# Four banks of the output projection begun early, and v rearranged in 2 KB rows

## The chip, the cores and the metric

The kernel runs on one core of a Trainium2 chip. The metric is the device time of one execution in microseconds, lower is better. Before the change three runs took 482.67, 484.89 and 485.15 us, median 484.89. TensorE (PE) multiplies 128x128 stationary weights by up to 512 moving columns into PSUM, which has eight banks of 128 x 512 float32 here; VectorE (DVE), ScalarE (ACT) and GpSimd (POOL) work beside it; nearly all DMAs are issued in order by SyncE (SP). Each engine runs its own instructions in a fixed order.

## The reference

One encoder layer on 1024 tokens of width 1024. A projection, two kinds of windowed attention, a gate, an output projection, a layer norm:

```python
h = x @ w_in                                   # columns split into eight sections
q_a, k_a, v_a, z_a, q_b, k_b, v_b, z_b = split(h)
# group a: 16 x 64 grid of tokens, 8 heads; each token sees an 8 x 16 window, with a bias per head
y_a = neighborhood_attention(q_a, k_a, v_a, rel_bias)
# group b: 8 query heads on 2 key heads, |i - j| <= 128, rotary positions, a sink logit per head
y_b = windowed_gqa_with_sink(rotary(q_b), rotary(k_b), v_b, sink)
mixed = concat([y_a * silu(z_a), y_b * silu(z_b)])
y = mixed @ w_out                              # 1024 x 1024
out = layer_norm(alpha * x + y) * gain + bias
```

## The kernel before

**Number format.** Float32 products are made from two halves. A tensor `r` is split into `h = round(r)` and `l = r - h`, and a product takes three matmuls: h·h, h·l and l·h. So each weight tile needs a cast (mostly ScalarE) and a subtraction (mostly GpSimd, 128x512) before PE can use it. `w_split` does this for the 42 tiles of `w_in` (`wr` raw, `wh`, `wl` split), `wo_split` for the 16 tiles of `w_out` (`wor` raw, `woh`, `wol`), `m_queue` and `m_split` for the eight 128-row slices `mh[e]`, `ml[e]` of the gated attention output.

**Stages.** First v is projected for all tokens (line 360) and scaled; `vt` holds its two float16 halves. Line 443 writes v of group a to DRAM as `vd`, 4 head pairs x 1024 tokens x 256 values (512 bytes a token and pair). Line 447 copies from it, in four DMAs, the column windows of the 16-row grid that four blocks of queries need, into `vwin0` to `vwin3` (24, 32, 32 and 24 columns of each grid row). Later `gather_v` (line 464) loads one block of one pair into `va`: partition = (row within a group of four, column), and four groups of rows side by side, 512 bytes each. That is once per pair and block, 16 loads, the last four in steps 112 to 118.

Before the step loop six projections (`zb0`, `z0`, `zb1`, `kb`, `qb0`, `z1`) run in full. `w_split(m)` also asks for the load of tile `m + 3` (line 137) once tile `m` is split. The scheduler orders the engines in this first part; the order in the step loop is that of the program.

**The step loop.** 128 units of attention (64 of group b, then 64 of group a; one unit is 128 queries of one head) run as a pipeline. Step `i` does the score matmuls of unit `i` (`stage_qk`, lines 531 and 532, into a bank with tag `s`, of which there are three), the masked copy and maximum on VectorE (line 538), the exponential on ScalarE (line 554), and for unit `i - 1` the split of the probabilities into float16 halves (ScalarE line 564, VectorE line 565) and their transpose by a DMA (line 568, into `tr`). Every fourth step, 8 steps late, the probabilities of four units are multiplied with v (`stage_pv`, line 593, 36 matmuls in group a) and four steps after that transposed and gated (`stage_ot`, lines 613 and 622).

Between these the loop fills PE with other work: the other 15 projections (48 matmuls each, line 290), then the first part of the output projection, called heads. `FILL_AT` gives the steps between which each piece of work is spread evenly, `FILL_N` its number of matmuls. The last projection is `z3`, 48 matmuls over steps 112 to 120. After it come five heads of nine matmuls: bank `(t, a)` holds 128 tokens `t` by 512 columns `a` of the output, and a head adds the slices e = 4, 5, 6 (group b), three matmuls each, into `(0, 0)`, `(1, 0)` (tag `pj`), `(3, 0)`, `(2, 0)`, `(0, 1)` (tag `s`), at steps 120 to 134. PE's matmuls of the output projection are all on line 702 (`out_mms`).

ScalarE, VectorE, GpSimd and SyncE have queues of small jobs (`enq`); in each step `pop` emits a fixed number of those whose predecessors are out. `wo_load` (line 656) asks for a tile of `w_out`; nine raw buffers exist. `WO_LD` gives the steps of the loads inside the loop (111 to 131), the splits come three steps later for tiles 0 to 5, `M_AT` the steps at which the slices e = 4, 5, 6 are split.

**The last stage** (`final`) loads tiles 9 to 14, splits the slices 7, 0, 1, 2, 3 and the tiles 6 to 15, begins banks `(1, 1)`, `(2, 1)`, `(3, 1)` with slices 4 to 6, adds the five slices to eight banks (t = 0 to 3), then does t = 4 to 7 in full. `residual` and `norm` (layer norm, in halves on VectorE, ScalarE and GpSimd) follow each row block; `norm_last` ends the kernel.

Of the kernel before, what the change touches and what calls it, by code (L numbers as in the profile page):

```python
# [9 lines left out]
F16 = mybir.dt.float16  # L10
# [7 lines left out]
GW = 64  # L18
ROWS = 16
# [8 lines left out]
         "k2", "q2", "z2", "k3", "q3", "z3"]  # L28
NPRO = 6
FILL = ORDER[NPRO:]  # L30
FILL_AT = [0, 8, 17, 25, 33, 41, 49, 57, 66, 74, 81, 89, 97, 105, 112, 120, 123, 126, 128, 131, 134]
ZTAG = {"z3": "zv", "zb3": "zc", "z2": "zs"}
X1AT = 4
VA_AT = [50, 53, 56, 59]
WO_TAG = ("wr", "wr", "wr", "wh", "wl", "wh", "wl", "wh", "wl")
M_AT = [105, 112, 115]
WO_LD = [111, 112, 113, 121, 122, 123, 129, 130, 131]
WIN0 = (0, 8, 24, 40)
WINW = (24, 32, 32, 24)
NKEY = tuple(12 * w for w in WINW)  # L40
# [6 lines left out]
def hybrid_block(ctx, tc, xT, x, wt, wv, wo, bias, sink, gain, lbias, cos, sin, bmask, out):  # L47
    nc = tc.nc
# [6 lines left out]
    dram = ctx.enter_context(tc.tile_pool(name="dram", bufs=1, space=bass.MemoryType.DRAM))  # L55
# [3 lines left out]
    def bank(tag):  # L59
        bufs = {"pj": 2, "s": 3, "t": 2, "ot": 1}[tag]  # L60
        return (ps1 if bufs == 1 else ps2).tile([128, 512], F32, tag=tag, name=f"ps_{tag}", bufs=bufs)

    vd = dram.tile([4, S, 256], F16, name="vd")
    vwin = [dram.tile([4, ROWS, WINW[b] * 256], F16, name=f"vwin{b}") for b in range(4)]

    def half_tile(name):
        return big.tile([128, 512], F32R, tag="big", name=name)
# [42 lines left out]
    def enq(eng, fn, *deps, prio=1):  # L110
        op = Op(eng, fn, deps, prio)
        if clock["step"] is None:
            op.emit()
        else:
            queues[eng].append(op)
        return op
# [15 lines left out]
    NH = 2 * len(ORDER)  # L132
# [26 lines left out]
    w_ops, stk_ops, load_ops = {}, {}, {}  # L159
# [113 lines left out]
    def new_group():  # L273
        if len(groups) >= 2:
            need(*groups[-2])
        return bank("pj")
# [35 lines left out]
    with ExitStack() as vctx:  # L312
# [131 lines left out]
                vd[:, 128 * t:128 * t + 128, :].rearrange("q p e -> p q e"),  # L444
                vt[:, 0:8].rearrange("p (q h) i e -> p q (h i e)", h=2))
        for b in range(4):
            nc.sync.dma_start(vwin[b], vd.rearrange("q (r c) e -> q r (c e)", c=GW)[
                :, :, 256 * WIN0[b]:256 * (WIN0[b] + WINW[b])])

# [8 lines left out]
    def gather_v(p, b):  # L460
        w = WINW[b]
        t = ap.tile([128, 4, 256], F16, tag="va", name=f"va{p}_{b}", bufs=5)
        bulk["last"] = bulk["step"]
        nc.sync.dma_start(t[:4 * w], vwin[b][p].rearrange("(g i) (c e) -> (i c) g e", g=4, e=256))
        va[p, b] = t

    def unit_list():
# [155 lines left out]

    pump_all(ORDER[1:NPRO])
    fill.extend(project(n) for n in FILL)
    FILL_N = [48] * len(FILL) + [9] * 5
    pumped = [0]

    def pump_to(u):
# [10 lines left out]
    def m_alloc(e, pair):  # L640
        mh[e], ml[e] = (stk(pair) for _ in range(2))
# [2 lines left out]
        hi(mh[e][:, sl], zt[e][:, sl])  # L644
        lo(ml[e][:, sl], zt[e][:, sl], mh[e][:, sl].bitcast(F32))

    WO_SEQ = [(e, a) for a in range(2) for e in EO[:3]] + [(e, a) for e in EO[3:] for a in range(2)]
    wo_parts = {}

    wo_raw = {}  # L650
# [1 line left out]
    def wo_load(n):  # L652
        if n < 16:
            raw = wp.tile([128, 512], F32, tag=WO_TAG[n % 9], name=f"wor{n}", bufs=3)
            e, a = WO_SEQ[n]
            nc.sync.dma_start(raw, wo[e, :, 512 * a:512 * a + 512])
            wo_raw[n] = raw
# [3 lines left out]
    def wo_split(n):  # L661
        def hi():
            wo_parts[n] = [half_tile(f"wo{w}{n}") for w in "hl"]
            copy = nc.vector.tensor_copy if clock["step"] is None else nc.scalar.copy
            copy(wo_parts[n][0], wo_raw[n])  # L665

        def lo():
            h, l = wo_parts[n]
            eng.tensor_sub(l, wo_raw.pop(n), h.bitcast(F32))  # L669

        eng, q = (nc.vector, "dve") if n % 3 == 2 else (nc.gpsimd, "pool")
        o = enq("act" if clock["step"] is not None else "dve", hi, load_ops.get(("wo", n)))
        o = enq(q, lo, o)
        wo_ops[n] = o
        if n >= 6:
            wo_load(n + 9)

    m_ops = {}

# [11 lines left out]
    def out_mms(t, a, ps, es, c=None):  # L691
        w = 512 if c is None else 256
        o = 0 if c is None else 256 * c
        ts, cs = slice(128 * t, 128 * t + 128), slice(o, o + w)
        ps = ps[:, o:o + w]
        for e in es:
            n = WO_SEQ.index((e, a))
            if n in wo_ops:
                need(wo_ops[n], *m_ops.get(e, ()))
            woh, wol = wo_parts[n]  # L700
            for i, (lh, rh) in enumerate(((mh[e], woh), (mh[e], wol), (ml[e], woh))):
                nc.tensor.matmul(ps, lh[:, ts], rh[:, cs],  # L702
                                 start=(e == EO[0] and i == 0), stop=(e == EO[-1] and i == 2))
                yield

    obank = {}

    def out_head(t, halves, tag):
        for a in halves:
            if tag == "pj":  # L710
                obank[t, a] = new_group()
                groups.append([])
            else:
                obank[t, a] = bank(tag)
        for e in EO[:3]:
            for a in halves:
                yield from out_mms(t, a, obank[t, a], [e])

    def final():
        actx.close()  # L720
        fp = ctx.enter_context(tc.tile_pool(name="fp", bufs=2, reuse_waits="tile"))
        eps = fp.tile([128, 1], F32, name="eps", bufs=1)
        nc.vector.memset(eps, EPS)
        m_alloc(7, "k")
        m_alloc(0, "k")
        m_alloc(1, "q")
        for e in (2, 3):
            mh[e] = fp.tile([128, S], F32R, name=f"mh{e}", bufs=1)
            ml[e] = fp.tile([128, S], F32R, name=f"ml{e}", bufs=1)
        for n in range(9, 15):  # L730
            wo_load(n)
        for e in EO[3:]:
            m_split(e, slice(0, 512), nc.scalar.copy, nc.vector.tensor_sub)
            for n in (WO_SEQ.index((e, 0)), WO_SEQ.index((e, 1))):
                wo_split(n)
        for e in EO[3:]:
            m_split(e, slice(512, S), nc.scalar.copy, nc.vector.tensor_sub)
        gb, bb = zslot("gb"), zslot("bb")
        nc.sync.dma_start(gb, gain.partition_broadcast(128))
# [62 lines left out]

        for t in range(NX):
            x_load(t)
        for t, a, tag in ((1, 1, "t"), (2, 1, "t"), (3, 1, "ot")):
            obank[t, a] = bank(tag)
            list(out_mms(t, a, obank[t, a], EO[:3]))
        for e in EO[3:]:
            for t in range(4):
                for a in range(2):  # L810
                    list(out_mms(t, a, obank[t, a], [e]))
                    if e == EO[-1]:
                        residual(t, a, obank[t, a])
                        if a == 0 and t > 0:
                            norm(t - 1)
                            x_load(t - 1 + NX)
# [13 lines left out]
        for c in range(2):  # L830
            ps = bank(next(tags) if c == 0 else "pj")
            list(out_mms(7, 1, ps, EO, c))
            residual(7, 1, ps, c)
        norm_last(7)

    fill.extend(out_head(t, (a,), tag) for t, a, tag in ((0, 0, "pj"), (1, 0, "pj"), (3, 0, "s"), (2, 0, "s"), (0, 1, "s")))
    clock["step"] = 0
    with tc.manual_schedule():
        for i in range(-LD, NU + LO):
            if 0 <= i + LD < NU:  # L840
                stage_load(units[i + LD])
            if i < 0:
                continue
            clock["step"] = i
            per, h = divmod(i, 16)
            bulk["step"] = i
            if i in VA_AT:
                gather_v(0, VA_AT.index(i))
            if i in WO_LD:
                n = WO_LD.index(i)  # L850
                load_ops["wo", n] = enq("sp", lambda n=n: wo_load(n))
            if i - 3 in WO_LD[:6]:
                wo_split(WO_LD.index(i - 3))
            if i in M_AT:
                m_queue(4 + M_AT.index(i))
            if bulk["last"] != i or (queues["sp"] and i - queues["sp"][0].born > 2):
                pop("sp", 1)
            if i < NU:
                u = units[i]
                if u[3] in (0, (0, 0)) and u[2] == 0:  # L860
                    need(*stk_ops[f"b{u[1]}" if u[0] == "b" else u[1]])
                stage_qk(u)
            q, m = divmod(i - LP - 3, 4)
            if m == 0 and 0 <= q - 1 < NU // 4:
                stage_ot(q - 1)
            if m == 0 and 0 <= q < NU // 4:
                stage_pv(q)
            if 0 <= i - LT < NU:
                stage_tr(units[i - LT])
            pump_to(i + F1)  # L870
            if m in (0, 2) and 0 <= q < NU // 4:
                g, p, j, h = quad(q)
                if g == "a" and j == 1 and p < 3:
                    gather_v(p + 1, 2 * h + m // 2)
            if m == 1 and 0 <= q < NU // 4:
                stage_on(q)
            pop("dve", ND if i < M_AT[1] else 2)
            if i < NU:
                stage_exp(units[i])
            pop("act", NA if i < M_AT[0] else 2)  # L880
            pop("pool", NP)
            pump_to(i + 1)
        pump(10 ** 6)
        need(*[op for q in queues.values() for op in q])
        clock["step"] = None
        final()


# [71 lines left out]
```

## Time and profile before

| what | us |
|---|---|
| median of three runs | 484.89 |
| the profiled execution, its own time | 485.24 |
| its span (first to last instruction) | 483.4 |
| PE busy in the span | 467.9 |
| v projection, on PE alone (line 360) | to about 62 |
| copies to `vwin` issued (line 447) | 102.84 to 105.62 |
| first scores (step 0) | 121.02 |
| scores of step 112 / 120 / 127 | 353.92 / 370.39 / 386.37 |
| end of the last matmul | about 475.4 |
| issue of the last store | 480.45 |

A window row of the profile gives, for a stretch of time, the busy time and number of instructions of each engine, the granted TensorE clock (1.00 is full speed), the mean busy share of the 16 DMA engines (it can exceed 1, where packets overlap) and the rate. A timeline row gives start, duration, engine, line, operation and tiles, and in brackets how long the engine had been idle and what released it. In a list of waits the three numbers are the total, how many times, and the longest. "DMA to landing" is from a DMA's issue to its last byte.

### The profile page before, as it was taken

How to read it: one execution, taken by the hardware profiler on the slowest of the kernel's cores; microseconds unless marked ns; L12 is line 12 of the kernel's file. 1: busy time of each engine (PE TensorE's matmuls, PEld its weight loads, DVE VectorE, ACT ScalarE, POOL GpSimd, SP SyncE). 2: the span in 40 equal slices, each digit the busy share in tenths (PEclk: the TensorE clock that was granted, in tenths of full speed). 3: DMA queues.
4: the chain of work that ended last, by engine and by line, in shares of the span. 5: the costliest groups of instructions: out<-in, count | busy, mean ns of one | idle time of the engine just before them, and what ended most of it. 6: DMA issues, size and time to landing. Idle time of an engine off the chain costs nothing.

```text
span 483.4 us, 9130 instructions
## 1 busy us (share of the span) xinstructions
PE 467.9 (97%) x3240; PEld 402.4 (83%) x3240; DVE 328.1 (68%) x780; ACT 251.2 (52%) x595; POOL 163.1 (34%) x151
## 2 busy tenths in 40 slices
PE   8999999999999999999999999999999599999993
PEld 6999988888788888888888888888888488888883
DVE  5728305868677878888788767767667549569445
ACT  5651123343577867777677766666777532012002
POOL 0030012596245247473215124113634116215423
PEclk9999999999999999999999999999999989999998
DMA  7871001477176666575999998999999988005612
GB/s 238 270 250 44 1 0 45 135 247 245 49 116 114 147 128 121 101 135 117 179 163 187 190 227 190 234 187 264 180 169 228 201 242 279 36 24 159 204 50 87
DMA packets 132381, 74.73 MB, mean 155 GB/s; under 512 B 101104, under 2 KB 117488, under 8 KB 132080
## 3 DMA queue, kind: packets, MB, share of 16 engines
q1 hardware_dynamic: 132192, 74.00, 67.0%
q8 instruction: 25, 0.41, 0.4%
q14 instruction: 20, 0.16, 0.1%
q10 hardware_dynamic: 144, 0.15, 0.1%
HBM read 43.72 MB, written 9.96 MB: 111 GB/s over the span
## 4 chain that ended last, share of the span: by engine, by line
PE 89%; DVE 4%; DMA 3%; ACT 2%; issue 1%; SPq 0%; ACTq 0%; DVEq 0%
PE ps_pj L290 44%; PE ps_s L702 7%; PE ps_t L593 7%; PE ps_t L702 5%; PE ps_pj L702 4%; PE ps_s L531 4%; PE ps_s L360 4%; PE ps_s L532 4%; PE ps_pj L360 3%; PE ps_t L360 3%; DMA tr<-split 2%; PE ps_ot L702 2%; PE ps_ot L613 1%; PE ps_ot L360 1%; DMA xraw<-in_xT 1%
## 5 line engine op out<-in xcount | busy, mean ns | idle before, releaser
L290 PE MATMUL ps_pj<-xh,wh 128*128 128x512 f32 x336 | 133.9, 398 | 0.8 <-ACT rp_raw L233 0.5
L290 PE MATMUL ps_pj<-xl,wh 128*128 128x512 f32 x336 | 131.9, 392 | 0.0
L290 PE MATMUL ps_pj<-xh,wl 128*128 128x512 f32 x336 | 131.6, 392 | 0.0
L152 POOL TENSOR_TENSOR wl<-wr,wh 128x512 fp32r<-128x512 f32 x42 | 55.5, 1323 | 170.7 <-ACT wh L148 129.6
L554 ACT ACTIVATE ps_s<-sn,nm 128x385 f32<-128x385 f32 (+3 forms) x128 | 70.5, 551 | 56.7 <-DVE nm L538 55.5
L565 DVE SCALAR_TENSOR_TENSOR split<-ps_s,split 128x384 f16<-128x384 f32 (+2 forms) x128 | 65.7, 513 | 17.9 <-ACT split L564 17.3
L290 PEld LDWEIGHTS ps_pj<-xh,wl 128*128 128x128 f32 x336 | 63.1, 188 | 13.3
L290 PEld LDWEIGHTS ps_pj<-xh,wh 128*128 128x128 f32 x336 | 63.2, 188 | 10.8 <-DVE z L262 0.7
L290 PEld LDWEIGHTS ps_pj<-xl,wh 128*128 128x128 f32 x336 | 63.2, 188 | 9.4
L564 ACT ACTIVATE split<-ps_s 128x384 f16<-128x384 f32 (+2 forms) x128 | 58.0, 453 | 10.4 <-DMA tr<-split 8.8
L538 DVE CUSTOM_DVE_ANT_0 sn<-ps_s,bm,nsk 128x384 f32<-128x384 f32 (+1 forms) x64 | 37.2, 582 | 18.9 <-PE ps_s L532 18.1
L538 DVE CUSTOM_DVE_ANT_0 sn<-ps_s,bias 128x288 f32<-128x288 f32 (+1 forms) x64 | 32.4, 506 | 25.3 <-PE ps_s L532 22.5
L531 PE MATMUL ps_s<-ks,qs 128*128 128x384 f32 (+2 forms) x128 | 41.4, 323 | 3.9 <-DVE split L565 3.9
L532 PE MATMUL ps_s<-ks,qs 128*128 128x384 f32 (+2 forms) x128 | 41.3, 322 | 0.0
L215 POOL CAST ks<-ks 64x512 fp32r<-64x512 f32 x40 | 27.2, 679 | 35.0 <-ACT ks L205 18.6
L593 PEld LDWEIGHTS <-tr 128*128 128x128 f16 (+1 forms) x1104 | 36.1, 99 | 2.4 <-issue 1.3
L531 PEld LDWEIGHTS ps_s<-ks,qs 128*128 128x128 f32 x128 | 24.1, 188 | 10.6 <-DVE split L565 5.4
L148 ACT CAST wh<-wr 128x512 fp32r<-128x512 f32 x42 | 25.7, 611 | 11.1 <-PE ps_pj L290 8.5
L532 PEld LDWEIGHTS ps_s<-ks,qs 128*128 128x128 f32 x128 | 24.2, 189 | 5.0
L669 POOL TENSOR_TENSOR wol<-wor,woh 128x512 fp32r<-128x512 f32 x11 | 15.8, 1443 | 35.5 <-ACT woh L665 19.0
L554 ACT ACTIVATION_READ_ACCUMULATOR ps_s<-sn,nm 128x1 f32 x128 | 24.1, 188 | 0.0
L799 POOL TENSOR_TENSOR xr<-xr,gb 128x512 f32<-128x512 f32 x7 | 9.1, 1294 | 42.3 <-ACT xr L796 42.3
(191 smaller groups left out, 865.9 us busy)
## 6 DMA issues: line engine op xcount, KB each, us to landing
wr<-in_wt SPq DMA_DIRECT2D x42, 256.0 KB, 3.1
bias<-in_bias SPq DMA_DIRECT2D x16, 288.0 KB, 4.0
wor<-in_wo SPq DMA_DIRECT2D x16, 256.0 KB, 4.8
xr<-in_x SPq DMA_DIRECT2D x8, 512.0 KB, 6.2
xraw<-in_xT SPq DMA_DIRECT2D x15, 256.0 KB, 4.3
out<-xr SPq DMA_DIRECT2D x14, 256.0 KB, 3.4
bias<-in_bias SPq DMA_DIRECT2D x8, 384.0 KB, 4.6
wvraw<-in_wv SPq DMA_DIRECT2D x7, 320.0 KB, 4.6
```

What stands on the lines that cost most here:

```text
L152: nc.gpsimd.tensor_sub(l, raws.pop(m), h.bitcast(F32))
L215: nc.gpsimd.tensor_copy(t[o, sl], t[a, sl])
L290: nc.tensor.matmul(ps, a[:, k % 4, :], b[half, k], start=(k == 0 and i == 0), stop=(k == KT - 1 and i == 2))
L360: nc.tensor.matmul(ps[:, :320], lh[t // 4, k][:, ts], rh[k][:, cs], start=(k == 0 and i == 0), stop=(k == KT - 1 and i == 2))
L531: nc.tensor.matmul(ps[:, :n], q, sl[0], start=True, stop=False)
L532: nc.tensor.matmul(ps[:, :n], q, sl[1], start=False, stop=True)
L538: nc.vector.tensor_tensor_reduce(sn[:, :n], ps[:, :n], bias_t, -1.0, init, op0=ALU.add, op1=ALU.min, accum_out=nm)
L554: nc.scalar.activation(pt[:, :m], sn[:, :m], AF.Exp, bias=nm, scale=-1.0, accum_out=sm[:, k:k + 1])
L564: nc.scalar.activation(hl[:, :m, 0, :c], src, AF.Copy, scale=PSCALE)
L565: nc.vector.scalar_tensor_tensor(hl[:, :m, 1, :c], src, PSCALE, hl[:, :m, 0, :c], op0=ALU.mult, op1=ALU.subtract)
L593: nc.tensor.matmul(ps[:, HD * m:HD * m + HD], a, b_, start=(i == 0), stop=(i == len(mms) - 1))
L702: nc.tensor.matmul(ps, lh[:, ts], rh[:, cs], start=(e == EO[0] and i == 0), stop=(e == EO[-1] and i == 2))
```

## The change

1. **v.** `vwin[b]` is now, for each pair, `4w` rows of 2 KB: row (i, c) holds the four row groups g side by side, so that `gather_v` reads one piece of 2 KB for each partition instead of four of 512 bytes. The copies into it are 16 instead of 4 (block x pair), and their pattern on both sides runs over g, i, c in this order, with pieces of 512 bytes at the destination.
2. **The last projection and the heads.** `z3` is spread over steps 112 to 123. The heads then go by pairs of banks: `(0,0)` and `(1,0)` (tag `pj`, steps 123 to 128), `(2,0)` and `(3,0)` (tag `s`, 128 to 132), slices 4 to 6; then slice 7 for all four (132 to 135): 18, 18 and 12 matmuls. The four other banks, `(0..3, 1)`, take slices 4 to 7 at the start of the last stage.
3. **Splits.** Slice 7 is split in the loop, from step 121. The order of the tiles (`WO_SEQ`) follows the four slices. Tiles 0 to 3 are split at steps 115, 116, 117 and 125 and tiles 4 to 7 at 132 and 133, by ScalarE and GpSimd (every third by VectorE); their loads are at 111, 112, 113, 122, 129, 129, 130, 130, and tiles 8 to 12 are loaded at 131 to 133. Loads now wait in the queue for the splits that free their buffers, and from step 129 SyncE takes three jobs a step instead of one. The last stage splits the tiles 8 to 15 and slices 0 to 3.
4. **The end.** 20 matmuls of 384 columns on two free banks are issued before `norm_last`; nothing reads their result.

```diff
-FILL_AT = [..., 105, 112, 120, 123, 126, 128, 131, 134]
+FILL_AT = [..., 105, 112, 123, 128, 132, 135]
-M_AT = [105, 112, 115]
-WO_LD = [111, 112, 113, 121, 122, 123, 129, 130, 131]
+M_AT = [105, 112, 115, 121]
+WO_AT = [115, 116, 117, 125, 132, 132, 133, 133]
+WO_LD = [111, 112, 113, 122, 129, 129, 130, 130, 131, 132, 132, 133, 133]
...
-    vwin = [dram.tile([4, ROWS, WINW[b] * 256], F16, name=f"vwin{b}") for b in range(4)]
+    vwin = [dram.tile([4, 4 * WINW[b], 4 * 256], F16, name=f"vwin{b}") for b in range(4)]
...
         for b in range(4):
-            nc.sync.dma_start(vwin[b], vd.rearrange("q (r c) e -> q r (c e)", c=GW)[
-                :, :, 256 * WIN0[b]:256 * (WIN0[b] + WINW[b])])
+            for q in range(4):
+                nc.sync.dma_start(
+                    vwin[b][q].rearrange("(i c) (g e) -> g i c e", i=4, g=4),
+                    vd[q].rearrange("(g i c) e -> g i c e", g=4, i=4)[:, :, WIN0[b]:WIN0[b] + WINW[b], :])
...
-        nc.sync.dma_start(t[:4 * w], vwin[b][p].rearrange("(g i) (c e) -> (i c) g e", g=4, e=256))
+        nc.sync.dma_start(t[:4 * w].rearrange("p g e -> p (g e)"), vwin[b][p])
...
-    FILL_N = [48] * len(FILL) + [9] * 5
+    FILL_N = [48] * len(FILL) + [18, 18, 12]
...
-    WO_SEQ = [(e, a) for a in range(2) for e in EO[:3]] + [(e, a) for e in EO[3:] for a in range(2)]
+    WO_SEQ = [(e, a) for a in range(2) for e in EO[:4]] + [(e, a) for e in EO[4:] for a in range(2)]
...
-        if n >= 6:
-            wo_load(n + 9)
+        if 4 <= n < 7:
+            load_ops["wo", n + 9] = enq("sp", lambda: wo_load(n + 9), o)
...
-    def out_head(t, halves, tag):
-        for a in halves:
+    def out_head(ts, es, tag):
+        for t in ts:
             if tag == "pj":
-                obank[t, a] = new_group()
+                obank[t, 0] = new_group()
                 groups.append([])
-            else:
-                obank[t, a] = bank(tag)
-        for e in EO[:3]:
-            for a in halves:
-                yield from out_mms(t, a, obank[t, a], [e])
+            elif tag is not None:
+                obank[t, 0] = bank(tag)
+        for e in es:
+            for t in ts:
+                yield from out_mms(t, 0, obank[t, 0], [e])
...
-        m_alloc(7, "k")
...
-        for n in range(9, 15):
-            wo_load(n)
-        for e in EO[3:]:
+        for e in EO[4:]:
             m_split(e, slice(0, 512), nc.scalar.copy, nc.vector.tensor_sub)
...
-        for t, a, tag in ((1, 1, "t"), (2, 1, "t"), (3, 1, "ot")):
-            obank[t, a] = bank(tag)
-            list(out_mms(t, a, obank[t, a], EO[:3]))
-        for e in EO[3:]:
+        for t, tag in ((0, "s"), (1, "t"), (2, "t"), (3, "ot")):
+            obank[t, 1] = bank(tag)
+            list(out_mms(t, 1, obank[t, 1], EO[:4]))
+        for e in EO[4:]:
...
+        pa, pb = bank("s"), bank("s")
+        for _ in range(2):
+            for i in range(4):
+                nc.tensor.matmul(pa[:, :384], mh[2][:, :128], wo_parts[14][0][:, :384], start=True, stop=True)
+            for i in range(6):
+                r = slice(64 * (i % 2), 64 * (i % 2) + 64)
+                nc.tensor.matmul((pa, pb)[i % 2][:, :384], mh[2][r, :128], wo_parts[14][0][r, :384],
+                                 start=True, stop=True)
         norm_last(7)
-    fill.extend(out_head(t, (a,), tag) for t, a, tag in ((0, 0, "pj"), (1, 0, "pj"), (3, 0, "s"), (2, 0, "s"), (0, 1, "s")))
+    fill.extend((out_head((0, 1), EO[:3], "pj"), out_head((2, 3), EO[:3], "s"), out_head(range(4), EO[3:4], None)))
...
-            if i in WO_LD:
-                n = WO_LD.index(i)
-                load_ops["wo", n] = enq("sp", lambda n=n: wo_load(n))
-            if i - 3 in WO_LD[:6]:
-                wo_split(WO_LD.index(i - 3))
+            for n in range(len(WO_LD)):
+                if WO_LD[n] == i:
+                    load_ops["wo", n] = enq("sp", lambda n=n: wo_load(n), w_ops.get(NH - 3 + n), wo_ops.get(n - 9))
+            for n in range(len(WO_AT)):
+                if WO_AT[n] == i:
+                    wo_split(n)
...
-                pop("sp", 1)
+                pop("sp", 1 if i < WO_LD[4] else 3)
```

More of the change, by code (lines that the diff above doesn't have):

```diff
@@ L30 @@
 FILL = ORDER[NPRO:]
-FILL_AT = [0, 8, 17, 25, 33, 41, 49, 57, 66, 74, 81, 89, 97, 105, 112, 120, 123, 126, 128, 131, 134]
+FILL_AT = [0, 8, 17, 25, 33, 41, 49, 57, 66, 74, 81, 89, 97, 105, 112, 123, 128, 132, 135]
 ZTAG = {"z3": "zv", "zb3": "zc", "z2": "zs"}
@@ L804, in final @@
             x_load(t)
-        for t, a, tag in ((1, 1, "t"), (2, 1, "t"), (3, 1, "ot")):
-            obank[t, a] = bank(tag)
-            list(out_mms(t, a, obank[t, a], EO[:3]))
-        for e in EO[3:]:
+        for t, tag in ((0, "s"), (1, "t"), (2, "t"), (3, "ot")):
+            obank[t, 1] = bank(tag)
+            list(out_mms(t, 1, obank[t, 1], EO[:4]))
+        for e in EO[4:]:
             for t in range(4):
```

## The prediction

> **What bounds the kernel now.** I read the page first: TensorE is busy almost everywhere, and the chain that ended last runs through it.
>
> ```profile
> PE 467.9 (97%) x3240; PEld 402.4 (83%) x3240; DVE 328.1 (68%) x780; ACT 251.2 (52%) x595; POOL 163.1 (34%) x151
> PE 89%; DVE 4%; DMA 3%; ACT 2%; issue 1%; SPq 0%; ACTq 0%; DVEq 0%
> ```
>
> So time is won only where PE stands still or runs slowly, and anything that holds PE back is lost in full. Second, the windows of the last steps and PE's waits there (columns: window, busy us and count of PE, PEld, DVE, ACT, POOL, granted clock, DMA share, GB/s).
>
> ```profile
> 354.00:370.00 16.00, 16.00 (x140) 13.62 (x139) 11.22 (x33) 12.74 (x34) 8.92 (x7) 1.00 1.10 218
> 370.00:386.40 16.40, 11.43 (x116) 8.96 (x114) 10.36 (x30) 9.31 (x28) 1.27 (x1) 0.94 1.15 204
> 386.40:391.20 4.80, 4.80 (x44) 3.98 (x44) 1.98 (x6) 4.12 (x10) 1.28 (x1) 0.50 0.79 182
> ...
> PE ps_s L531 <- DVE split L565: 3.9, 2, 2.9
> ```
>
> The reader sees PE full until 370 us, then 5.0 us idle in 16.4, then 4.8 us at a granted clock of 0.50, which loses 2.4 us. Together 7.4 us: the most that the rearranged late steps can win. PE waits for a score bank, which waits for the split of an earlier unit, which waits for its transpose. Third, therefore, SyncE's queue there.
>
> ```profile
> 366.70 0.57 SPq L508 DMA_DIRECT2D bias<-in_bias  x1
> 367.38 1.21 SPq L568 DMA_TRANSPOSE tr<-split  x1
> 368.64 0.58 SPq L464 DMA_DIRECT2D va<-vwin  x1
> 369.32 1.56 SPq L568 DMA_TRANSPOSE tr<-split  x1
> 370.93 0.57 SPq L508 DMA_DIRECT2D bias<-in_bias  x1
> 371.60 1.21 SPq L568 DMA_TRANSPOSE tr<-split  x1
> 372.87 0.57 SPq L464 DMA_DIRECT2D va<-vwin  x1
> ```
>
> SyncE issues without a pause: eight transposes from 358.08 to 375.6 us are 2.19 us apart, while the steps come every 2.06 us (scores of step 112 at 353.92, of step 120 at 370.39). Fourth, the place where v is rearranged in DRAM (SyncE, then ScalarE, PE and windows).
>
> ```profile
> 102.84 2.78 SPq L447 DMA_DIRECT2D vwin<-vd  x4
> 106.67 24.00 SPq L137 DMA_DIRECT2D wr<-in_wt  x5
> ...
> 120.74 0.62 ACT L148 CAST wh<-wr 128x512 fp32r<-128x512 f32 x1
> 121.27 0.58 ACT L233 COPY rp_raw<-ps_pj 128x512 f32<-128x512 f32 x1
> ...
> 121.90 0.50 PE L290 MATMUL ps_pj<-xh,wh 128*128 128x512 f32 x1 [0.49 <-ACT rp_raw L233]
> ...
> 91.50:94.00 2.50, 2.50 (x12) 2.07 (x12) 1.11 (x2) 1.17 (x3) 2.22 (x3) 1.00 1.04 314
> 103.30:118.00 14.70, 14.70 (x66) 12.17 (x66) 12.99 (x17) 5.47 (x9) 12.83 (x15) 1.00 0.92 299
> ```
>
> The four vwin copies keep the DMA engines full from 103.3 to 118.0 us. The weight load issued at 106.67 lands 11.9 us later (the longest landing of that line), at 118.6: behind them. ScalarE casts it at 120.74, and in its fixed order the copy of a projection bank (121.27), for which PE waits at 121.90, stands behind that cast. There is about 2 us between the end of the vwin data and a stall of PE.
>
> **The change part by part.** *Late steps.* From the scores of step 112 to those of step 127 before took 386.37 - 353.92 = 32.45 us. PE issues 62 matmuls of 512 columns there instead of 70 (48 of z3 and 14 of the heads instead of 22), at 0.229 us from start to start 14.2 us; 15 score pairs at 0.32 are 4.7, four blocks of probabilities times v and transposes at 1.5 are 6.0; sum 24.9. Steps 112 to 120 keep SyncE's eight transposes, three biases, four gathers and weight loads, so I leave them at 16.5 us although PE needs 13.6. Steps 120 to 127 hold 27 matmuls (6.2), 7 score pairs (2.2), two blocks (3.0): 11.4 us; SyncE needs only 7 x 1.27 + 0.66 + 0.6 = 10.2, as two weight loads have left. A new wait comes in: both pj banks are now opened at step 123, and the second needs the evacuation of z3's second half at once; before, that took from 370.39 to 375.75 us, hidden by the first bank's nine matmuls. Three matmuls (0.7) and a score pair cover it now; I take 1.0 (0 to 3). Scores of step 127 then come at 16.5 + 11.4 + 1.0 = 28.9, 3.55 us earlier. The eight matmuls come later, +1.8. Idle time is spread in pieces under 1 us, where before 2.89 us in one piece came ahead of the slow clock, so I take the 2.4 of slow clock as gone, less 0.3 inside the 32.45: -2.1.
>
> Weights 4 to 7 are now loaded behind the last transpose. That was issued 3.5 us after the last scores; +1.25, three more issues of 0.6, landing 4.8 (its row), a ScalarE cast 0.6, GpSimd's three subtractions in turn at 1.28 to 1.5: the last is ready 13.5 us after the last scores. PE wants it after 34 matmuls (7.8), two v blocks (2.1), transposes (1.3), scores (0.3) and nine head matmuls (2.1): 13.6. Just in time; 0.5 (0 to 2). Late steps together: -3.55 + 1.8 - 2.1 + 0.5 = -3.35, say -3.5 with a trifle for the shorter gathers; bounds -7.4 and +1.
>
> *At nothing:* m7's two casts (0.62) replace two weight casts on ScalarE, and its subtractions find POOL busy 1.27 us of 16.4. The four output banks at full depth have 48 matmuls (11 us) before the first weight split in the last stage is wanted, where 27 were. The 20 matmuls of 384 columns at the end (0.18 us apart by the score rows) run 3.6 us from 475.1 to 478.7, while the last store is issued at 480.45; at half clock they end at 482.3, still inside the span of 483.4. The matmuls taken into the heads are the same work elsewhere.
>
> *v in 2 KB pieces.* Gathers: 112 pieces instead of 448 on average, off PE's path; 0 to -0.5 us, inside the trifle. Their price is the copies: 16 instead of 4, in 112 columns x 16 rows x 4 pairs = 7168 pieces of 512 B, 3.67 MB as before. Issue: 16 x 0.65 = 10.4 us, until 113.3, hidden since the data run to 118 anyway. What decides is on how many DMA engines they run. Before, each had 64 equal rows (q and r are evenly spaced); every other transfer here has 96 or 128 and the windows show all 16 engines filled (share 0.92 to 1.04). The new pattern leads with g, four entries, on both sides; no row shows a lead under 64. Bounds: sixteen engines, 14.7 us as now, cost 0; or a transfer handed out by its leading entries, thus four engines. Then: vd's copies, also of 512 B, moved 314 to 346 GB/s on 16 engines (half-microsecond windows at 92 to 93 us: 345), 21.6 GB/s or 23.7 ns a piece on one; 7168 / 4 x 23.7 ns = 42.5 us, from 103.3 to 145.8. The weight load behind them has a quarter of its rows on those engines and lands about 1.2 us later, 147; cast 0.6, bank copy 0.6, PE goes on at 148.7 instead of 121.9: +26.8. A PE idle that long comes back at the slow clock: +2.4 by the row at 386.4. Sum +29.2. By the vwin rate (299 GB/s: 27.4 ns) the copies take 49.1 us, +6.6; at the best windows (389 GB/s) 37.7, -4.8; if the bank copy is put ahead of the cast PE stops only at 130.2, -8.
>
> I take four engines: four leading entries can't be dealt out evenly to sixteen, and nothing in the trace argues for a second level of splitting. The Trainium skill, "DMA: Bandwidth & Descriptors", section "Why a DMA increments its semaphore by 16 and not by 1", says the same outright: the number of engines is the largest one up to 16 that divides the slowest dimension of both sides, and it is the lowest-numbered ones that are used. By that rule the sum is 510.9; by the rows' share of one it is 481.7. No run here shows a transfer with such a lead.
>
> **Sum.** The profiled execution took 485.24 us (span 483.4 and 1.8 around it), 0.35 above the median of 484.89. 485.24 - 3.5 + 29.2 = 510.9, by the median 510.6.
>
> **The rivals.** *Sixteen engines*, the other side: only the late steps tell, 484.89 - 3.5 = 481.4 (477.5 to 486). For it: the same bytes ran at share 0.92 before. Against: the leading four. It decides as long as the vwin data end by about 120 us. *Sixteen engines and no late gain*: SyncE paces steps 112 to 127 as before (2.19 us a transpose) and the evacuation at 123 costs 3: 484.9 + 1 = 486. *Four engines, but two weight loads are issued ahead of the copies*: the next one is wanted at about 144, with the second projection after 130; 147 + 2 - 144 is 5, so 484.9 - 3.5 + 5 = 486.5. Against: the copies waited only for vd, ready at 102.8, and the load for a buffer freed at 106.65.
>
> **Chances.** Four engines 0.60; sixteen with gain 0.24; sixteen without 0.08; four with loads ahead 0.08. Predicted 510.6; its own range 495 to 521 (-8 - 4.8 - 3 and +6.6 + 4). The whole range reaches from 478 to 521. Half a per cent, 2.4 us, is about what can be told from no change: faster 0.25, same 0.07 (parts of the last two and of the second), slower 0.68.
>
> **What would show it.** Right: DMA share near 0.25 from 104 to 145 us, SyncE's weight loads landing past 140, PE idle from 122 with the wait at a bank copy or a cast of wr, slow clock after it; then the same step spacing as before, and in the last steps no idle over 1 us and no slow clock. Wrong: vwin data done by 120 us and PE full there. The late part is wrong if the scores of step 127 come over 31 us after those of step 112, or if PE waits over 2 us for wol ahead of the four heads.

## The result and the profile after

| kernel | median of the runs, us | lowest to highest |
|---|---|---|
| before (6 runs beside the change) | 483.91 | 482.09 to 485.41 |
| after (6 runs) | 514.35 | 512.44 to 517.58 |

The ratio is 1.0643, 95% interval 1.0597 to 1.0689: 30.4 us slower by the medians. The profiled execution of after took 517.58 us (span 515.8), the longest of its six, 3.2 us above the median. The page again first: total busy time, the row of PE in 40 slices of 12.9 us, the chain that ended last.

```profile
PE 474.3 (92%) x3260; PEld 407.1 (79%) x3260; DVE 324.6 (63%) x776; ACT 253.4 (49%) x597; POOL 165.6 (32%) x153
...
PE   8999999994039999999999999999999798999996
...
PE 77%; SPq 9%; DMA 6%; DVE 4%; ACT 2%; issue 2%; POOL 1%; ACTq 0%; POOLq 0%
```

PE has a hole in the tenth to twelfth slice (4, 0, 3), 116 to 155 us, that wasn't there. The chain has a new member, SyncE's issuing queue, with 9% of the span (46 us); before it had 0%. The place is where v is rearranged, so its rows come next: SyncE, then ScalarE and PE from the timeline (start, duration, engine, line; in brackets the idle time and its releaser), then the windows.

```profile
103.62 39.77 SPq L449 DMA_DIRECT2D vwin<-vd  x16
143.49 15.74 SPq L138 DMA_DIRECT2D wr<-in_wt  x5
...
149.32 0.62 ACT L149 CAST wh<-wr 128x512 fp32r<-128x512 f32 x1 [27.96 <-DMA wr<-in_wt]
149.85 0.58 ACT L234 COPY rp_raw<-ps_pj 128x512 f32<-128x512 f32 x1
...
150.48 0.79 PE L291 MATMUL ps_pj<-xh,wh 128*128 128x512 f32 x1 [28.42 <-ACT rp_raw L234]
```

```profile
106.00:122.00 16.00, 16.00 (x72) 13.06 (x70) 13.82 (x16) 5.90 (x10) 11.65 (x12) 1.00 0.29 87
122.00:143.00 21.00, 0.06 (x1) 0.00 (x0) 0.16 (x1) 0.00 (x0) 0.00 (x0) 0.57 0.29 87
...
145.00:146.00 1.00, 0.00 (x0) 0.00 (x0) 0.00 (x0) 0.00 (x0) 0.00 (x0) 0.50 0.29 87
146.00:147.00 1.00, 0.00 (x0) 0.00 (x0) 0.00 (x0) 0.00 (x0) 0.00 (x0) 0.50 0.76 204
...
150.50:155.50 5.00, 5.00 (x12) 3.94 (x13) 4.56 (x9) 2.13 (x3) 0.79 (x1) 0.50 0.17 54
```

The reader sees the DMA share at 0.29 and 87 GB/s through both long windows and on to 146 us, while PE, VectorE, ScalarE and GpSimd stand still from 122 us on. SyncE needs 39.77 us to issue the 16 copies and asks for the next weight tile only then, at 143.49. Its cast follows at 149.32, the copy of the projection bank behind it, and PE goes on at 150.48, at a granted clock of 0.50 for another 5.0 us.

The last steps, same views as before (window rows of after for steps 112 to 120, steps 120 to 127 and the 4.8 us behind them):

```profile
384.22:398.76 14.54, 13.71 (x127) 11.01 (x125) 10.37 (x31) 11.84 (x32) 8.70 (x7) 1.00 0.93 186
398.76:416.49 17.73, 13.90 (x119) 11.52 (x119) 10.36 (x33) 10.63 (x29) 2.71 (x3) 0.90 1.07 200
416.49:421.30 4.81, 4.81 (x54) 4.04 (x53) 2.35 (x7) 2.37 (x7) 1.27 (x1) 1.00 1.06 123
```

PE's waits in after that are new there:

```profile
PE ps_t L596 <- DMA tr<-split: 2.3, 3, 1.1
PE ps_s L705 <- POOL wol L672: 1.6, 2, 0.9
PE ps_pj L705 <- DVE z L263: 1.4, 1, 1.4
```

Steps 112 to 120 became shorter (14.54 us; before 16.47), steps 120 to 127 longer (17.73; before 15.98), with 3.8 us of idle PE in short pieces and the slow clock (0.90) now inside them. Behind them the clock is full, where it was 0.50 before. SyncE's rows there (timeline):

```profile
401.99 0.57 SPq L511 DMA_DIRECT2D bias<-in_bias  x1
402.66 1.22 SPq L571 DMA_TRANSPOSE tr<-split  x1
403.93 0.58 SPq L467 DMA_DIRECT2D va<-vwin  x1
404.62 4.10 SPq L571 DMA_TRANSPOSE tr<-split  x3
```

SyncE's rows still follow each other without a pause. By the starts of the scores, the time of after against before parts as follows (us): step 1 came at 162.04 instead of 131.72, 30.3 later; step 112 was 30.3, step 127 30.1 later; the rest of the span took 99.31 instead of 97.03. Of the 32.4 us between the two spans, 30.3 are thus there by the second scores, and the other 2.1 come later, behind step 127.

### The profile page after: what moved, and what is told of

Same layout as the page of the kernel before. It is cut to its first block, busy times and chain, and to the rows that moved or that the text cites. A ratio compares the mean times of both kernels' runs of the same rounds, so it can differ in the third digit from the quotient of the medians.

```text
span 515.8 us, 9183 instructions
## 1 busy us (share of the span) xinstructions
PE 474.3 (92%) x3260; PEld 407.1 (79%) x3260; DVE 324.6 (63%) x776; ACT 253.4 (49%) x597; POOL 165.6 (32%) x153
## 4 chain that ended last, share of the span: by engine, by line
PE 77%; SPq 9%; DMA 6%; DVE 4%; ACT 2%; issue 2%; POOL 1%; ACTq 0%; POOLq 0%
PE ps_pj L291 36%; SPq L449 8%; PE ps_t L596 6%; PE ps_s L705 5%; PE ps_pj L705 5%; PE ps_t L705 4%; PE ps_s L361 4%; PE ps_s L534 4%; PE ps_s L535 4%; PE ps_t L361 3%; PE ps_pj L361 3%; DMA tr<-split 2%; PE ps_ot L705 2%; DVE v L440 2%; DMA vd<-vt 1%
## 5 line engine op out<-in xcount | busy, mean ns | idle before, releaser
L291 PEld LDWEIGHTS ps_pj<-xh,wh 128*128 128x128 f32 x336 | 63.8, 190 | 38.3 <-ACT rp_raw L234 28.6
L568 DVE SCALAR_TENSOR_TENSOR split<-ps_s,split 128x384 f16<-128x384 f32 (+2 forms) x128 | 65.5, 512 | 18.9 <-ACT split L567 18.3
L541 DVE CUSTOM_DVE_ANT_0 sn<-ps_s,bias 128x288 f32<-128x288 f32 (+1 forms) x64 | 32.3, 505 | 23.8 <-PE ps_s L535 22.6
```

Of the source, the lines that this page charges most:

```text
L291: nc.tensor.matmul(ps, a[:, k % 4, :], b[half, k], start=(k == 0 and i == 0), stop=(k == KT - 1 and i == 2))
L541: nc.vector.tensor_tensor_reduce(sn[:, :n], ps[:, :n], bias_t, -1.0, init, op0=ALU.add, op1=ALU.min, accum_out=nm)
L568: nc.vector.scalar_tensor_tensor(hl[:, :m, 1, :c], src, PSCALE, hl[:, :m, 0, :c], op0=ALU.mult, op1=ALU.subtract)
```

## The experiments

The theory: the copies run on four DMA engines, since their pattern leads with four; they last 42 us, and the weight load behind them stops PE. The first rival: it is not the lead but the 16 issues or the 512-byte pieces; the second: the late steps have a share in it. Times are medians; each ratio is to before, run on the same chip in the same session.

### v_only and late_only: the two halves of the change

```diff
# v_only: before, and from the change only
-    vwin = ... [4, ROWS, WINW[b] * 256]
+    vwin = ... [4, 4 * WINW[b], 4 * 256]      with its 16 copies and gather_v
# late_only: after, and of the change taken back
-    vwin, its 16 copies, gather_v
+    those of before
```

> The kernel before with the 2 KB rows of v alone (16 copies that lead with g = 4, and their gathers); late steps as before. Four-engine theory: the copies' leading four decides, so this alone loses what the whole change lost at the start: the copies run at 87 GB/s and DMA share 0.29 from about 104 to 145 us, PE waits some 28 us for a bank copy, time 484 + 30 = 514 us (512 to 517). Rival (the late steps carry the loss, or the two parts hit each other): under 490 us.

> The changed kernel with v copied and gathered as before, so the new late steps alone. Recorded sum: -3.5 us, 480.4 us. Rival (SyncE's and the DMA engines' pace holds steps 112 to 127, and matmuls put off are paid later): 484 us, -1 to +2; scores of step 127 come 32 us after those of step 112, as in both kernels, where the sum had 28.9.

v_only: 513.93 us (510.73 to 514.81), ratio 1.0604 [1.0562, 1.0646]. late_only: 484.91 us (482.67 to 487.19), ratio 1.0015 [0.9994, 1.0036]. The longest of PE's waits in v_only, then SyncE's timeline:

```profile
PE ps_pj L290 <- ACT rp_raw L233: 28.6, 1, 28.6
```

```profile
104.23 40.01 SPq L448 DMA_DIRECT2D vwin<-vd  x16
144.35 15.73 SPq L137 DMA_DIRECT2D wr<-in_wt  x5
```

The rearrangement of v carries the whole loss, by the same wait. The late steps bring nothing that can be measured, where 3.5 us had been forecast. Their two windows in late_only (steps 112 to 120, 120 to 127):

```profile
353.37:367.92 14.55, 13.72 (x127) 11.01 (x126) 10.38 (x31) 11.85 (x32) 8.70 (x7) 1.00 1.24 183
367.92:384.62 16.70, 12.43 (x120) 10.35 (x120) 10.01 (x31) 10.39 (x29) 2.71 (x3) 1.00 0.98 210
```

The pattern of after without the copies: the first eight steps are 1.9 us shorter than before, the next seven 0.7 longer, with 4.3 us of idle PE. So steps 120 to 127 get longer without the new layout of v too; how much of the 17.73 us in after is due to v, one profile of each doesn't tell.

### big_lead4, big_lead8, big_lead16: the leading number alone

These three start from before and keep its layout and gathers; only the copies are split, 16 instead of 4, by block and pair, with pieces of 12 to 16 KB (as many bytes as before). What leads the pattern on both sides is 4, 8 or 16.

```diff
-            nc.sync.dma_start(vwin[b], vd.rearrange(...)[...])
+            for q in range(4):
+                nc.sync.dma_start(                                   # big_lead4
+                    vwin[b][q].rearrange("(g i) x -> i g x", i=4),
+                    vd[q].rearrange("(g i c) e -> i g (c e)", g=4, i=4)[:, :, cols])
# big_lead8:  "(h i) x -> i h x", i=8
# big_lead16: vwin[b][q]  <-  vd[q].rearrange("(r c) e -> r (c e)", c=GW)[:, cols]
```

> The kernel before with its four copies made 16, each one pair and block, whose pattern leads with i (four) on both sides; pieces stay at 12 to 16 KB. Four-engine theory: four engines again, share about 0.25 to 0.29, 75 to 96 GB/s, 3.67 MB take 38 to 49 us, time 510 to 522 us. Rival (piece size decides): 16 engines' rate, 484 us.

> As big_lead4, with the grid rows taken as two halves of eight, so that the pattern leads with eight on both sides; pieces of 12 to 16 KB, 16 copies. If the engines are as many as the lead: about 208 GB/s (twice the 104 of big_lead4), DMA share about 0.5, 3.67 MB in 18 us, done at about 121 us, weight load at 122 to 123, PE waits 1 to 4 us: 486 to 489 us. Rivals: four engines for any lead under 16, 507 us; all engines, 484 us.

> Control for big_lead4: the kernel before with its four copies made 16, pieces of 12 to 16 KB as there, but each pattern leads with the 16 grid rows. Four-engine theory (the lead decides): all engines, 16 issues of 0.6 to 0.9 us, data done by about 119 us, 484 us (483 to 487). Rival (16 copies in a row fill SyncE's queue whatever the lead): 500 us or more.

| lead | time, us | ratio | issue of the 16 copies, us | rate, GB/s | DMA share | longest wait of PE for a bank copy, us |
|---|---|---|---|---|---|---|
| 4 | 506.77 | 1.0458 [1.0411, 1.0504] | 20.53 | 106 | 0.26 | 20.0 |
| 8 | 489.27 | 1.01 [1.0066, 1.0134] | 13.49 | 217 | 0.52 | 4.9 |
| 16 | 484.24 | 1.0008 [0.9983, 1.0034] | 10.44 | 303 | 0.92 | 0.5 |

Window rows of the three, in this order, from within the copies:

```profile
104.00:120.00 16.00, 16.00 (x73) 13.23 (x72) 13.64 (x16) 6.18 (x11) 12.45 (x13) 1.00 0.26 106
```

```profile
108.00:112.00 4.00, 4.00 (x19) 3.34 (x18) 3.93 (x4) 0.00 (x0) 3.31 (x4) 1.00 0.52 217
```

```profile
108.00:112.00 4.00, 4.00 (x19) 3.34 (x18) 3.77 (x4) 0.13 (x1) 3.14 (x3) 1.00 0.92 303
```

The share is a mean over 16 engines: 4/16 is 0.25, 8/16 is 0.50. The number of issues does not make the loss: 16 issues at a lead of 16 cost nothing that can be measured. The lead makes most of it, and the wait grows as the lead falls: at a lead of 4, large pieces lose 22.6 us where v_only lost 29.7. Pieces of 512 bytes add about 7 us at that lead; at a lead of 16 they bring no long wait (lead16, below). With 506.77, big_lead4 came out under its forecast, since the large pieces went at 106 GB/s where 75 to 96 had been expected; its profiled execution took 502.24 us, 4.5 below the median, so its rows may be somewhat short. big_lead8 came out just above its own forecast (486 to 489 us, waits of 1 to 4). The Trainium skill, "DMA: Bandwidth & Descriptors", section "Why a DMA increments its semaphore by 16 and not by 1", has the number of engines as the largest up to 16 that divides the slowest dimension on both sides; these three shares (0.26, 0.52, 0.92) agree with it.

big_lead4 also parts two causes that after joins. SyncE and ScalarE there (timeline):

```profile
101.98 20.53 SPq L448 DMA_DIRECT2D vwin<-vd  x16
124.43 25.19 SPq L137 DMA_DIRECT2D wr<-in_wt  x5
...
139.71 0.62 ACT L148 CAST wh<-wr 128x512 fp32r<-128x512 f32 x1 [19.55 <-DMA wr<-in_wt]
```

The weight load is issued at 124.43 and cast 15.3 us later: here it waits in the engines behind the copies' data. In after it was cast 5.8 us after its issue: there SyncE itself was held. So an earlier issue alone would hardly have saved after; no run tests that by itself.

### lead16: the whole change with a lead of 16

`vd` is stored by row group, so that a copy of one block and one row group leads with (pair, row) = 16; layout of `vwin`, pieces of 512 bytes and 16 copies stay.

```diff
-    vd = dram.tile([4, S, 256], ...)
+    vd = dram.tile([4, 4, 256, 256], ...)         # row group, pair, token, value
...
+            for g in range(4):
+                nc.sync.dma_start(
+                    vwin[b].rearrange("q (i c) (g e) -> g (q i) c e", i=4, g=4)[g],
+                    vd[g].rearrange("q (i c) e -> (q i) c e", i=4)[:, WIN0[b]:WIN0[b] + WINW[b], :])
```

> The changed kernel with vd kept in DRAM in another order (row group, pair, row, column), so that the 16 copies, again of 512-byte pieces and as many bytes, lead with 16 on the source and 384 on the destination. Four-engine theory: 16 engines, copies done within 15 us (about 300 to 345 GB/s), no wait of 28 us on PE, time as late_only within 2 us. Rival (512-byte pieces from DRAM to DRAM are slow in themselves, or 16 copies are too many for SyncE): copies past 130 us and PE waits, 495 to 514 us.

490.19 us (488.18 to 490.65), ratio 1.0118 [1.0093, 1.0142]: 24 us of the 30 are gone, but it is still 5.3 us above late_only, which it had been expected to match. SyncE's timeline in lead16:

```profile
104.90 7.15 SPq L449 DMA_DIRECT2D vwin<-vd  x8
112.15 24.20 SPq L138 DMA_DIRECT2D wr<-in_wt  x7
```

The longest of PE's waits, and a window row from within the copies:

```profile
PE ps_s L534 <- DVE qs L184: 3.6, 1, 3.6
```

```profile
103.00:107.00 4.00, 4.00 (x19) 3.33 (x18) 3.36 (x7) 1.49 (x3) 3.66 (x6) 1.00 1.02 290
```

The copies do run on all engines (1.02, 290 GB/s). The expectation missed their order: a copy by row group needs two stores of v instead of all eight, so it is ready earlier, and the scheduler put all 16 ahead of two weight loads that stood between the stores before (98.30 and 101.89 us; here 112.15). Step 1 came at 138.9 us instead of 131.72. In the prediction's last rival the loads stood ahead of the copies; here the order is turned round. spread16, below, has the same layout with the copies out of the way, and this loss is gone.

### spread4, v_spread16, spread16: the copies in the step loop

Each of the 16 copies is issued in the loop, one every second step from 2 to 32. spread4 has the lead of 4 of the change on v_only; v_spread16 the lead of 16 on the same base; spread16 is the whole change with the lead of 16.

```diff
+            if 2 <= i < 34 and i % 2 == 0:
+                nc.sync.dma_start(...)             # one of the 16 copies
```

> v_only with the same 16 copies that lead with four, but issued one in every second step of the loop (steps 2 to 32), behind the weight loads of the first projections. Theory (four engines cost nothing in themselves; the loss is that the weight load and with it ScalarE's cast and bank copy stand behind 40 us of copies): each copy takes about 2.5 us on four engines while a pair of steps takes 3.5, the transposes wait up to 2.5 us, seven tr buffers hide it: 484 to 488 us. Rival (a copy on four engines costs its time wherever it stands): 500 us or more, PE waiting for transposes in steps 2 to 34.

> The kernel before with 2 KB rows of v alone, copies leading with 16 and issued one in every second step of the loop. No copy stands before a weight load, so what is left is the worth of the shorter gathers: my theory, that steps 112 to 127 are paced by the DMA engines and SyncE, gives -1 to -2 us (v_only had 30.2 us from the scores of step 112 to those of 127 where before had 32.5): 482.5 us. Rival (gathers were hidden anyway): 484 us.

> The whole changed kernel with copies leading with 16, one in every second step of the loop. If the late steps gain only where the DMA engines are relieved, the two parts together give -2 to -4 us: steps 112 to 127 in 29 to 30 us as in lead16, 481.5 us. Rival (late steps give nothing in any case): as v_spread16.

| kernel | time, us | ratio |
|---|---|---|
| spread4 | 506.54 | 1.0457 [1.0419, 1.0495] |
| v_spread16 | 483.83 | 0.9984 [0.996, 1.0007] |
| spread16 | 484.6 | 1.0005 [0.9984, 1.0027] |

For spread4 the expectation fell: the transposes were to wait up to 2.5 us, hidden by seven `tr` buffers. Its rival came instead, a copy on four engines that costs its time wherever it stands. Window rows of the same length, before first, then spread4:

```profile
135.00:220.00 85.00, 85.00 (x689) 73.33 (x688) 68.27 (x192) 63.99 (x165) 45.14 (x37) 1.00 0.66 125
```

```profile
135.00:220.00 85.00, 69.38 (x494) 57.93 (x493) 51.33 (x142) 47.65 (x122) 30.48 (x25) 0.92 0.95 130
```

PE's longest waits in spread4, then a copy and two transposes behind it in SyncE's timeline, and two such transposes in v_spread16:

```profile
PE ps_t L590 <- DMA tr<-split: 13.8, 7, 3.3
PE ps_s L528 <- DVE split L562: 5.0, 4, 2.2
```

```profile
156.82 0.61 SPq L846 DMA_DIRECT2D vwin<-vd  x1
157.54 3.63 SPq L565 DMA_TRANSPOSE tr<-split  x2
```

```profile
144.92 2.60 SPq L565 DMA_TRANSPOSE tr<-split  x2
```

PE waits for transposes. Two of them behind a copy take SyncE 3.63 us here and 2.60 in v_spread16; the longest single one takes 4.21 us in the steps with copies, where the longest in v_spread16 takes 2.16. A copy (229 KB on average) takes its four engines 2.64 us at the 87 GB/s of after, and two transposes take SyncE 2.42 at 1.21 (one alone, as in before): 5.06 us for every two steps, 81 us for the 32 steps with copies. These 32 steps took 83.4 us by the starts of their scores (132.90 to 216.33) and 61.4 before (131.72 to 193.13). So copy and transposes, one after the other, would fill nearly the whole stretch. Steps 1 to 112 took 22.8 us more (245.04 for 222.20). That a transpose waits for the four busy engines is inferred from this sum: no row shows a single engine, and copies that hold SyncE itself would give the same. With the lead of 16 the same schedule costs nothing (0.9984), so the lead decides here too.

v_spread16 was to gain 1 to 2 us by the shorter gathers (482.5); its gain can't be told from none. spread16 is the change without its fault, and it is no faster than before; 481.5 had been expected. Its profiled execution took 481.53 us, 3.1 below the median of its twelve, and has 29.20 us in steps 112 to 127, so its rows show the late steps at their best.

### nobias_late, nobias_early, poolq: what paces the last steps

All three change the last group-a pair only. The first two leave out its six bias loads (on spread16 and v_spread16), and VectorE reads the band mask in place of the bias; poolq, on spread16, has GpSimd issue these six and the last four gathers.

```diff
# nobias_late, nobias_early
-            if half == 0 and b != 2:
+            if half == 0 and b != 2 and p < 3:
# poolq
-                nc.sync.dma_start(bt..., ...)
+                (nc.gpsimd if p == 3 else nc.sync).dma_start(bt..., ...)       # gather_v likewise
```

> spread16 (new late steps, 2 KB gathers on 16 engines) without the six bias loads of the last 32 units of group a, which read the band mask in SBUF in place of their bias: 1.9 MB and six SyncE issues less from step 108 on. Theory (SyncE and the DMA engines pace steps 112 to 127, and that is why the new late steps win nothing): scores of step 127 come 25.5 to 27.5 us after those of step 112 (PE's own work is 24.9), and the kernel gains 2 to 4 us on spread16: 481 us. Rival (the late gain is lost behind step 127, in put-off matmuls and waits for split weights): under 1 us gained.

> The same loads left out of v_spread16, which has the late steps of before. There PE has 70 matmuls in steps 112 to 127 instead of 62 (26.7 us of its own work). Theory: 27 to 29 us for these steps, about 1.5 to 3 us gained: 481.5 us; and with the transposes no longer late, the new late steps (nobias_late) are the better by 0 to 2 us, since the eight matmuls that they put off come back after step 127. Rival (the old late steps lose by their own order of banks): 30 us or more for these steps, 484 us.

> spread16 with the last six bias loads and the last four gathers of v issued by GpSimd instead of SyncE: the same bytes, ten issues less (6 us) on SyncE's queue in steps 108 to 122. If SyncE's issue time is the pace: like nobias_late, 2 to 4 us gained on spread16. If the DMA engines' throughput is: the same time as spread16 within 1 us, 484.5 us.

| kernel | time, us | ratio | steps 112 to 127 in its profile, us |
|---|---|---|---|
| nobias_late | 481.8 | 0.9934 [0.9905, 0.9963] | 27.24 |
| nobias_early | 482.82 | 0.9958 [0.9934, 0.9982] | 29.57 |
| poolq | 485.88 | 1.0034 [1.0006, 1.0062] | 31.45 |

The windows of nobias_late, steps 112 to 120 and 120 to 127:

```profile
355.39:370.06 14.67, 13.88 (x128) 11.04 (x126) 10.48 (x31) 12.38 (x34) 8.82 (x7) 1.00 0.89 169
370.06:382.63 12.57, 11.82 (x119) 10.13 (x119) 10.07 (x31) 9.69 (x27) 2.59 (x3) 1.00 0.91 188
```

nobias_late came out as expected; nobias_early gained less than forecast, and poolq is 1.3 us above spread16, where 2 to 4 us of gain or the same time had been expected. Without the six loads the last seven steps take 12.57 us (14.65 in spread16), what the prediction had given them (12.4); PE has no wait for `tr` in the list, where spread16 has 2.9 us. Taking the issue of these loads and of the gathers from SyncE (poolq) brought nothing, and 3.4 us of waits for `tr` remained. So it looks as if the bytes on the DMA engines, not SyncE's time, held the transposes back. Three things stay open: these are single profiles; poolq's gathers came in bursts and took 5 to 6 us to land, so its schedule differs in more than the queue, and the intervals of nobias_late and nobias_early overlap, so it isn't shown that the late change profits more from the missing loads.

Late steps in the profiles of all kernels that do the whole work (one each, means in us):

| | 112 to 120 | 120 to 127 | 127 to the end |
|---|---|---|---|
| seven kernels with the late steps of before (before, v_only, big_lead4, big_lead8, big_lead16, spread4, v_spread16) | 16.5 | 15.2 | 96.3 |
| five with those of after (after, late_only, lead16, spread16, poolq) | 14.6 | 16.1 | 98.2 |
| difference | -1.9 | +0.9 | +1.9 |

The sum is +0.9, in keeping with late_only's ratio (+0.7 us, -0.3 to +1.7). The first column varies by at most 0.2 within a row, the second by 2.3 and 3.3, the third by about 2, so only the first is sharp.

## Why the prediction was right, and where not

The forecast of 510.6 us met 514.35 (ratio 1.0643 [1.0597, 1.0689]).

**Four engines: right.** Share 0.29 in after; 0.26, 0.52 and 0.92 at leads of 4, 8 and 16.

**Duration of the copies: right, in part by luck.** 87 GB/s on four engines are 21.75 GB/s each, 23.5 ns for 512 bytes (23.7 taken from vd's copies). SyncE has issued the last copy at 143.4 and the last data end at about 146.0 (145.8). But the price came from stores out of SBUF on all engines. Pieces of 512 bytes from DRAM to DRAM on all engines, in lead16, went at 290 GB/s, about 28 ns each, near the 27.4 that the prediction had as its upper bound; that four engines go faster each was not foreseen.

**Who waits: right, with one term wrong behind it.** The order load, cast, bank copy, PE held. PE went on at 150.48, 28.6 us later than before, where 26.8 were forecast. The term "16 x 0.65 = 10.4 us", taken as hidden, failed: the issue took 39.77 us, with a median of 2.8 us for one copy, about as long as its data need (229 KB on average at 87 GB/s: 2.6 us). The weight load was thus not in the queue behind the data but not issued at all. It moved the sum little, because big_lead4 shows the load to land behind the data anyway; it would have mattered for any other work of SyncE. The cast began 3.3 us after the end of the data, where 1.2 were forecast. The forecast's own sum is half a microsecond too long here: 147 and twice 0.6 are 148.2, not 148.7.

**Slow clock: right.** The clock of 0.50 lasts 5.0 us, which loses 2.5; 2.4 were forecast. Step 1 is 30.3 us late, 28.6 of them the wait, so only 1.7 are left beside it: at 130 us PE in before lost about half a microsecond at a bank (`PE ps_pj L290 <- DVE z L262`, 0.3 in its list of waits) that after doesn't lose. Together 30.3 against 29.2.

**The late term: mis-sized, by 4 us.** -3.5 forecast, +0.7 [-0.3, +1.7] measured in late_only. By the prediction's own sign (over 31 us from the scores of step 112 to those of step 127) it is wrong in after (32.27) and in late_only (31.25). Four of its parts came out otherwise.

- Steps 112 to 120 were left at 16.5 us as paced by SyncE; they took 14.6, near PE's own need of 13.6. The first window row of the prediction had shown the bound of before: PE is busy there for 16.00 of 16.00 us, with 140 matmuls, and after has 127. So the view of SyncE "without a pause" did not show a bound.
- Steps 120 to 127 were given 12.4 us, from PE's work and SyncE's issues; they took 14.4 to 17.7, and nobias_late reached 12.57 only without the bias loads, so the sum seems to have lacked the DMA engines' own work (what is left open above stands there).
- The slow clock of 2.4 us was to vanish. Behind step 127 it did (1.00 in all five), but in after and poolq it came in the steps ahead (0.90). Nor was it a fixed price of the old order: big_lead4 and v_spread16 have those late steps and 1.00 behind step 127.
- The waits varied: 1.4 us for the second bank in after and late_only and 0.6 in lead16 and spread16 (1.0 taken); 1.6 us for `wol` in after, 1.1 in late_only, at most 0.2 in lead16 and spread16 (0.5 taken).

The +1.8 of the put-off matmuls fits the +1.9 behind step 127, but that difference holds clock and waits too, so it isn't measured by itself.

**The rivals.** "Sixteen engines and no late gain" is what spread16 ran (484.6; 486 forecast). "Sixteen engines" with gain (481.4) isn't reached by the median of any kernel that does all the work. "Loads ahead" came up turned about in lead16. **Hidden as said:** the 20 matmuls at the end ran from 507.48 to about 510.7, before the last store's issue at 512.74.

## What to carry to other kernels

Read the leading dimension of both sides of every transfer, DRAM to DRAM too: a layout that is better for the reader can be paid for by a writer that uses a quarter of the engines, and reordering the dimensions so that 16 lead took the loss away here, as long as the order of the transfers stayed (big_lead16) or the copies were out of the way (spread16). Price such a transfer three times: its data, the issuing engine that it holds, and every later transfer behind it (in spread4 the transposes). When the idle time of a stage is to be won, sum up the load of the DMA engines beside that of PE and the issuing queue; a queue without pauses need not be the bound, and a window in which PE is busy throughout names PE.

## What was unexpected of the hardware

- SyncE is held while few engines drain its copies: 16 issues took 10.44 us at a lead of 16, 13.49 at 8, 20.53 at 4 (pieces of 12 to 16 KB) and 39.77 at 4 with pieces of 512 bytes.
- One engine moved more where fewer worked: 26.5 GB/s each at a lead of 4 and 27.1 at 8 (106/4, 217/8), but 18.9 at 16 (303/16). The windows hold some other transfers too, so these are near values.
- A partial use of the engines cost time far from its place: in spread4 nothing waited for the copies themselves, and they cost 22.8 us by the waits for transposes behind them.
